# Pieces of four in place of two in the halved feed-forward blocks of a two-layer diffusion trunk

## The chip, the core and the metric

The program runs on one core of a Trainium2 chip. Its time is device microseconds (us) from start to end of one execution. The engines are TensorE (PE, with its weight loads as PEld), VectorE (DVE), ScalarE (ACT), GpSimd (POOL) and SyncE (SP); DVE, ACT, POOL and SP each take their instructions in a fixed order.

## The reference, cut to what matters

The reference is a trunk of two layers over 512 latent and 256 context tokens, 1024 wide, in float32. Each layer is a half feed-forward step, a mixer and a second half feed-forward step. Only the feed-forward step matters here:

```
def _swiglu(h, w1, w3, w2):                     # h: tokens x 1024, D_FF = 2816
    return (jax.nn.silu(h @ w1) * (h @ w3)) @ w2

x = x + 0.5 * gate * _swiglu(modulate(rmsnorm(x)), w1, w3, w2)      # the same for the context y
```

The modulation vectors (shift, scale, gate, nine per layer) are products of `silu(c)` with the columns of `w_mod`, 1024 x 9216 per layer, and need that matrix once.

## The kernel before, in words

Everything is kept transposed: features on the 128 partitions, tokens along the row. The hidden width 2816 is 22 tiles of 128, counted by `f`; the model width is 8 tiles, counted by `dt`. Each float32 product is three matmuls on high and low parts (`mm3`, lines 162 to 167): `wh` by `xh`, `wh` by `xl`, `wl` by `xh`. The parts of a weight tile come from `parts` (line 582) and `split` (line 157): a load from DRAM into a `raw` buffer (SP, line 579), a cast to `wh` on ACT, a subtraction to `wl` on DVE. There are five `raw` buffers and four pairs of `wh` and `wl`, and the weights are prepared in one fixed order, up to four tiles ahead.

Two of the four feed-forward blocks, the second of layer 0 and the first of layer 1, are "halved" (`HALVED`, line 40; `ffn_halved`, line 808). They follow each other in time. In them a hidden tile from `f` = 4 on is made by `up_halved` (line 752): seven products of 12 matmuls each, 384 columns wide, in place of eight of that size, by a scheme with sums and differences of weights (lines 611 to 618, on DVE) and of tokens (the 24 tiles `T`, slots of 512 columns that live through the whole block). ACT copies partial results out of PSUM (`half`, line 774), DVE adds them (lines 788, 795), and the two factors are multiplied and split into `g` (lines 796 to 805). Between a copy and the next product into the same PSUM tile stands one other product; the copies stand in ACT's order behind the activation of line 789, which needs DVE's line 788.

A block runs in pieces. A piece makes `n` hidden tiles (the up stage) and then multiplies them by its part of `w2` into all 8 `dt` of both token groups (the down stage). The downs of a piece stop at PSUM: ACT scales each result into a slot `xpart` (line 229) and POOL adds it in DRAM to the parked stream (`xkept`, line 231), 16 adds a piece. Only the last piece adds in SBUF. Before the change the pieces are 2 and 2 (tiles 0 to 3, not halved), seven of 2 (tiles 4 to 17), and one of 4 (tiles 18 to 21). In a down stage two `dt` of both groups, four PSUM tiles, go together: first the products with the piece's first hidden tile for all four, then with its second one, then the four evictions. The PSUM has 8 such tiles, and all activations share 45 slots (line 86).

Beside this the modulation vectors of the next use are made on DVE by `mod_chunks` (line 364), on a clock of its own that counts matmul time: one chunk of `w_mod`, 512 KB, is loaded by SP into one of two `wm` buffers (line 371) and used by four DVE instructions (`macc`, lines 319 and 321); after every four chunks DVE folds the sums (lines 329, 330). Where a chunk's instructions fall among the others on DVE is settled when the program is built, as is the order on each engine. A `raw` or `wm` load waits on SP until its buffer is free, and those behind it wait too.

Of the kernel before, what the change touches and what calls it, by code (L numbers as in the profile page):

```python
# [22 lines left out]
NF = DFF // P  # L23
PIECES = (4, 4, 4, 4, 2, 4)
# [16 lines left out]
HK, HN, SUB, WHOLE = KD // 2, NT // 2, 2, 4  # L41
# [3 lines left out]
def per_block(n):  # L45

    return 2 if n * P * 2 <= 1024 else 1
# [34 lines left out]
class Kernel:  # L82
# [443 lines left out]
    def weight_order(self):  # L526

        ins = self.ins

        def halved(l, s):  # L530
            f0 = 0
            for npc in PIECES:
                w2 = ins["w2"][l, s, :, f0 * D : (f0 + npc) * D].rearrange("p (d f n) -> p d f n", d=KD, f=npc)
                sub = npc if f0 + npc == NF else SUB
                for a in range(0, npc, sub):
                    for f in range(f0 + a, f0 + a + sub):
                        both = [ins["w13"][l, s, f, :, m * 1024 : (m + 1) * 1024] for m in range(2)]
                        if f < WHOLE:
                            yield from both
                        else:  # L540
                            yield both
                    per = 8 // sub
                    for d in range(0, KD, per):
                        yield w2[:, d : d + per, a : a + sub]
                f0 += npc

        def ffn(l, s):
            f0 = 0
            for npc in PIECES:
                for f in range(f0, f0 + npc):  # L550
                    for m in range(2):
                        yield ins["w13"][l, s, f, :, m * 1024 : (m + 1) * 1024]
                n = npc * P * per_block(npc)
                for c in range(f0 * D, (f0 + npc) * D, n):
                    yield ins["w2"][l, s, :, c : c + n]
                f0 += npc

        for l in range(DEPTH):
            yield from (halved if (l, 0) in HALVED else ffn)(l, 0)
            for i in range(4, 8) if l < DEPTH - 1 else range(4):  # L560
                yield ins["w_feat"][l, i]
            for i in range(4) if l < DEPTH - 1 else range(4, 8):
                yield ins["w_feat"][l, i]
            for i in range(4):
                yield ins["w_tok"][l, i]
            for i in (10, 11, 12, 13, 8, 9, 14, 15, 16, 17):
                yield ins["w_feat"][l, i]
            for i in range(2):
                for dt2 in range(KD // 2):
                    yield ins["w_out"][l, i, dt2]  # L570
            yield from (halved if (l, 1) in HALVED else ffn)(l, 1)
# [236 lines left out]
    def ffn_halved(self, l, s, h, starts, grps, ends, done):  # L808
        nc = self.nc
        idx = 2 * s  # L810
        accs = {}
        T = {i: [[None] * HK for _ in range(2)] for i in (2, 3, 4)}
        f0 = 0
        while f0 < NF:
            g = self.empty()
            n = SUB if f0 < NF - PIECES[-1] else PIECES[-1]
            last = f0 + n == NF
            per = 8 // n

            def load():  # L820
                for st in (CTX, LAT):
                    self.load_x(st, self.kept[st])

            if f0 < WHOLE:
                if f0 == 0:
                    ws = {f: self.w13() for f in range(n)}
                    for grp in starts[:-1]:
                        self.up(ws, range(n), h, g, grp)
                    self.need(starts[-1])
                    task = self.spawn(self.differences(h, T), 1.0)  # L830
                for f in range(n):
                    if f0:
                        ws = {f: self.w13()}
                    for grp in grps if f0 else starts[-1:]:
                        self.up(ws, [f], h, g, grp)
                if f0 + n == WHOLE:
                    self.drain(task)
                    self.first_difference(h)
            else:
                for f in range(n):  # L840
                    self.up_halved(f, h, T, g, load if last and f == n - 1 else None)
            w2 = []

            def down(dt, grp, ps, fs):
                self.products([(ps, w2[dt // per], dt % per * n * P + fs[0] * P)], g, grp, fs, fs[0] == 0, fs[-1] == n - 1)

            if last:
                w2 = [self.weights() for _ in range(KD // per)]
                for grp in ends:
                    for dt in range(KD):  # L850
                        ps = self.psum("down")[:, : grp[2]]
                        down(dt, grp, ps, range(n))
                        xd = self.xs(dt, grp)
                        nc.vector.scalar_tensor_tensor(xd, ps, self.gate(l, idx, grp[0], dt), xd, op0=ALU.mult, op1=ALU.add)
                        self.square(dt, grp, accs)
                    done(grp, accs)
            else:
                for d in range(0, KD, 2):
                    if d % per == 0:
                        w2.append(self.weights())  # L860
                    these = [(dt, grp, self.psum("down")[:, : grp[2]]) for grp in grps for dt in (d, d + 1)]
                    for fs in ((0,), (1,)):
                        for dt, grp, ps in these:
                            down(dt, grp, ps, fs)
                    for dt, grp, ps in these:
                        self.add_kept(dt, grp, ps, self.gate(l, idx, grp[0], dt))
            f0 += n
# [675 lines left out]
```

## Time and profile before

| | |
|---|---|
| time, median of 3 runs | 2588.97 us (2588.43 to 2592.09) |
| time of the profiled execution | 2592.09 us |
| its span | 2590.3 us |
| PE busy | 2529.6 us, 98% |
| DVE, ACT, POOL busy | 70%, 39%, 11% |
| second feed-forward block of layer 0, halved | 905 to 1433 us |
| first feed-forward block of layer 1, halved | 1433 to 1985 us |

PE is busy nearly all the time. A stage of the halved blocks is best read as a stretch of its own: two stretches with the same number of matmuls, one longer than the other, show what the longer one lost.

### The profile page before, as it was taken

The page shows a single profiled execution, that of the slowest core. Times are in us where ns is not written, and L with a number is a line of the kernel's source. Part 1 is how long each engine was busy: PE and PEld are TensorE (multiplying, and loading weights), DVE is VectorE, ACT ScalarE, POOL GpSimd, SP SyncE. Part 2 cuts the span into 40 slices and gives each one's busy share as a digit, 9 for nine tenths or more (in the row PEclk, how much of TensorE's full clock was granted, in tenths as well). Part 3 has the DMA queues.
Part 4 walks back from the last instruction along what each step waited for, and adds up shares of the span by engine and source line. Part 5 has one row for each costly group of instructions (what it writes and reads, how often), then busy time and mean ns, then how long its engine had stood idle before and what let it go on. Part 6 is the DMA issues. An engine that isn't in the chain of part 4 may idle for free. (4 is left out here: it accounts for less than half of the span.)

```text
span 2590.3 us, 36708 instructions
## 1 busy us (share of the span) xinstructions
PE 2529.6 (98%) x14002; PEld 2246.6 (87%) x14002; DVE 1811.2 (70%) x3390; ACT 1015.7 (39%) x1780; POOL 276.6 (11%) x316
## 2 busy tenths in 40 slices
PE   8999999999999999999999999999999999999998
PEld 4888888888888888999899889989998888888887
DVE  6957767747977677788788858758777786633345
ACT  3211211223335444555454445545544263422223
POOL 0000000000000122422320132322310001000000
PEclk9999999999999999999999999999999999999999
DMA  7533433422222745787775457776663334232231
GB/s 273 161 108 122 139 122 114 130 74 100 85 79 60 198 106 130 180 204 180 168 196 187 110 111 195 162 179 179 145 159 122 114 97 119 91 98 98 94 102 41
DMA packets 149265, 345.37 MB, mean 133 GB/s; under 512 B 15712, under 2 KB 54112, under 8 KB 149088
## 3 DMA queue, kind: packets, MB, share of 16 engines
q1 hardware_dynamic: 101088, 276.94, 32.5%
q0 software_dynamic: 44928, 61.89, 15.0%
q10 hardware_dynamic: 3072, 4.20, 0.6%
q8 instruction: 109, 1.79, 0.3%
q14 instruction: 68, 0.56, 0.1%
HBM read 263.27 MB, written 75.50 MB: 131 GB/s over the span
## 5 line engine op out<-in xcount | busy, mean ns | idle before, releaser
L159 ACT CAST wh<-raw 128x1024 fp32r<-128x1024 f32 (+1 forms) x400 | 400.7, 1004 | 863.6 <-PE up L165 329.8
L160 DVE TENSOR_TENSOR wl<-raw,wh 128x1024 fp32r<-128x1024 f32 (+1 forms) x400 | 464.3, 1164 | 338.2 <-ACT wh L159 325.3
L164 PE MATMUL up<-h,wh 128*128 128x512 f32 (+2 forms) x1920 | 663.0, 347 | 21.9 <-ACT half L774 15.7
L165 PE MATMUL up<-h,wh 128*128 128x512 f32 (+2 forms) x1920 | 662.3, 345 | 0.2
L166 PE MATMUL up<-h,wl 128*128 128x512 f32 (+2 forms) x1920 | 661.0, 345 | 0.0
L231 POOL DMA_DIRECT2D xkept<-xpart x312 | 276.4, 1550 | 1904.2 <-ACT xpart L229 1595.0
L164 PE MATMUL down<-g,wh 128*128 128x256 f32 (+1 forms) x1264 | 425.7, 345 | 8.3 <-ACT xpart L229 4.3
L165 PE MATMUL down<-g,wh 128*128 128x256 f32 (+1 forms) x1264 | 431.2, 343 | 0.0
L166 PE MATMUL down<-g,wl 128*128 128x256 f32 (+1 forms) x1264 | 428.2, 341 | 0.4 <-DVE wl L160 0.4
L164 PEld LDWEIGHTS up<-h,wh 128*128 128x128 f32 x1920 | 365.7, 191 | 59.3 <-ACT half L774 17.9
L165 PEld LDWEIGHTS up<-h,wh 128*128 128x128 f32 x1920 | 366.6, 191 | 33.1 <-DVE h L515 0.7
L166 PEld LDWEIGHTS up<-h,wl 128*128 128x128 f32 x1920 | 366.2, 191 | 31.3
L321 DVE SCALAR_TENSOR_TENSOR macc<-wm,sc,macc 128x512 f32<-128x512 f32 x462 | 320.2, 746 | 56.5 <-DMA wm<-in_w_mod_dram 56.3
L164 PEld LDWEIGHTS down<-g,wh 128*128 128x128 f32 x1264 | 236.8, 190 | 41.0 <-ACT g L159 8.3
L165 PEld LDWEIGHTS down<-g,wh 128*128 128x128 f32 x1264 | 240.5, 190 | 28.1 <-DVE g L160 1.7
L166 PEld LDWEIGHTS down<-g,wl 128*128 128x128 f32 x1264 | 239.6, 190 | 28.3 <-DVE wl L160 0.6
L229 ACT ACTIVATE xpart<-down,gate 128x256 f32<-128x256 f32 (+1 forms) x288 | 152.5, 585 | 72.1 <-PE down L166 69.9
L663 DVE TENSOR_TENSOR silu<-silu,up 128x256 f32<-128x256 f32 (+1 forms) x84 | 48.5, 579 | 159.0 <-PE up L166 159.0
L164 PE MATMUL up<-t,wh 128*128 128x384 f32 x432 | 145.2, 336 | 0.3 <-ACT half L774 0.2
L166 PE MATMUL up<-t,wl 128*128 128x384 f32 x432 | 144.4, 334 | 0.0
L165 PE MATMUL up<-t,wh 128*128 128x384 f32 x432 | 144.4, 334 | 0.0
L700 DVE SCALAR_TENSOR_TENSOR x<-down,gate,x 128x512 f32<-128x512 f32 (+1 forms) x152 | 95.0, 634 | 65.9 <-PE down L166 65.2
(210 smaller groups left out, 3298.3 us busy)
## 6 DMA issues: line engine op xcount, KB each, us to landing
raw<-in_w_dram SPq DMA_DIRECT2D x260, 512.0 KB, 3.8
wm<-in_w_mod_dram SPq DMA_DIRECT2D x128, 512.0 KB, 4.3
xkept<-xpart POOLq DMA_DIRECT2D x160, 256.0 KB, 9.3
xkept<-xpart POOLq DMA_DIRECT2D x152, 128.0 KB, 8.6
raw<-in_w_feat_dram SPq DMA_DIRECT2D x36, 512.0 KB, 3.6
xkept<-x SPq DMA_DIRECT2D x44, 256.0 KB, 3.2
x<-xkept SPq DMA_DIRECT2D x44, 256.0 KB, 6.3
wm<-in_w_mod_dram SPq DMA_DIRECT2D x32, 256.0 KB, 5.5
```

What stands on the lines that cost most here:

```text
L159: self.nc.scalar.copy(hi, src)
L160: self.nc.vector.tensor_sub(lo, src, hi.bitcast(F32))
L164: nc.tensor.matmul(out, wh, xh, start=start, stop=False, skip_group_check=shared)
L165: nc.tensor.matmul(out, wh, xl, start=False, stop=False, skip_group_check=shared)
L166: nc.tensor.matmul(out, wl, xh, start=False, stop=stop, skip_group_check=shared)
L229: self.nc.scalar.activation(part, ps, AF.Copy, scale=gate)
L231: self.nc.gpsimd.dma_start(self.kept[st][:, c0 : c0 + n], part, accum_op=ALU.add)
L321: self.nc.vector.scalar_tensor_tensor(acc[v], raw, s, acc[v], op0=ALU.mult, op1=ALU.add)
L663: nc.vector.tensor_mul(t, t, ps[f, 1])
L700: nc.vector.scalar_tensor_tensor(xd, ps, self.gate(l, idx, grp[0], dt), xd, op0=ALU.mult, op1=ALU.add)
```

## The change

The halved tiles are done in pieces of `PIECES[1:]`, that is 4, 4, 4, 2 and 4, behind the two pieces of 2 that are not halved. A block then has 7 pieces in place of 10, 6 of them with adds in DRAM in place of 9; over both blocks there are 96 evictions and 96 adds fewer. The matmuls are the same ones. In the down stage of a piece of four, the first group of products is that of the first three hidden tiles, the second that of the fourth. `weight_order` gives the weights in the new order, with `w2` in tiles of two `dt` by four `f`, which are contiguous in a row, in place of four `dt` by two `f`.

```
--- before.py
+++ after.py
@@ -531,7 +531,7 @@
             f0 = 0
             for npc in PIECES:
                 w2 = ins["w2"][l, s, :, f0 * D : (f0 + npc) * D].rearrange("p (d f n) -> p d f n", d=KD, f=npc)
-                sub = npc if f0 + npc == NF else SUB
+                sub = SUB if f0 < WHOLE else npc
                 for a in range(0, npc, sub):
                     for f in range(f0 + a, f0 + a + sub):
                         both = [ins["w13"][l, s, f, :, m * 1024 : (m + 1) * 1024] for m in range(2)]
@@ -811,9 +811,8 @@
         accs = {}
         T = {i: [[None] * HK for _ in range(2)] for i in (2, 3, 4)}
         f0 = 0
-        while f0 < NF:
+        for n in (SUB,) * (WHOLE // SUB) + PIECES[1:]:
             g = self.empty()
-            n = SUB if f0 < NF - PIECES[-1] else PIECES[-1]
             last = f0 + n == NF
             per = 8 // n
 
@@ -859,7 +858,7 @@
                     if d % per == 0:
                         w2.append(self.weights())
                     these = [(dt, grp, self.psum("down")[:, : grp[2]]) for grp in grps for dt in (d, d + 1)]
-                    for fs in ((0,), (1,)):
+                    for fs in (range(n - 1), range(n - 1, n)):
                         for dt, grp, ps in these:
                             down(dt, grp, ps, fs)
                     for dt, grp, ps in these:
```

The order of the instructions is the same as before up to the first halved tile of layer 0, and again behind the second halved block; between these it differs as follows. (From line 815 on, the changed kernel's lines are lower by one.)

On PE, in the first down stage behind halved tiles, the products with the last hidden tile begin as follows before (`g_1489` and `g_1508` hold that tile; 24 matmuls of the stage stand ahead of the first one with it):

```order
L164 MATMUL down_9672<-g_1485_9435,wh_9537 128x512
L165 MATMUL down_9672<-g_1486_9436,wh_9537 128x512
L166 MATMUL down_9672<-g_1485_9435,wl_9538 128x512
L164 MATMUL down_9629<-g_1489_9460,wh_9537 128x256
L164 MATMUL down_9630<-g_1489_9460,wh_9537 128x256
L164 MATMUL down_9631<-g_1508_9577,wh_9537 128x512
L164 MATMUL down_9632<-g_1508_9577,wh_9537 128x512
L165 MATMUL down_9629<-g_1490_9461,wh_9537 128x256
```

and with the change (`g_1538` and `g_1557` hold the fourth tile; 36 matmuls of the stage stand ahead):

```order
L164 MATMUL down_9919<-g_1534_9733,wh_9841 128x512
L165 MATMUL down_9919<-g_1535_9734,wh_9841 128x512
L166 MATMUL down_9919<-g_1534_9733,wl_9842 128x512
L164 MATMUL down_9916<-g_1538_9758,wh_9841 128x256
L165 MATMUL down_9916<-g_1539_9759,wh_9841 128x256
L166 MATMUL down_9916<-g_1538_9758,wl_9842 128x256
L164 MATMUL down_9917<-g_1538_9758,wh_9841 128x256
```

The last hidden tile is needed 36 matmuls into the stage in place of 24.

On DVE, at the start of the up stage of tile 14 in layer 0 (1239 us in the trace), before: `wl_11768` is the last weight tile of tile 14, `wm_` are chunks of `w_mod`, line 788 is the first addition for tile 14:

```order
L160 TENSOR_TENSOR wl_11768<-raw_11517,wh_11767 128x512
L319 TENSOR_SCALAR macc_11730<-wm_11476,sc 128x512
L319 TENSOR_SCALAR macc_11731<-wm_11476,sc 128x512
L321 SCALAR_TENSOR_TENSOR macc_11730<-wm_11476,sc,macc_11730 128x512
L321 SCALAR_TENSOR_TENSOR macc_11731<-wm_11476,sc,macc_11731 128x512
L321 SCALAR_TENSOR_TENSOR macc_11730<-wm_11732,sc,macc_11730 128x512
L321 SCALAR_TENSOR_TENSOR macc_11731<-wm_11732,sc,macc_11731 128x512
L321 SCALAR_TENSOR_TENSOR macc_11730<-wm_11732,sc,macc_11730 128x512
L321 SCALAR_TENSOR_TENSOR macc_11731<-wm_11732,sc,macc_11731 128x512
L160 TENSOR_TENSOR wl_11841<-raw_11565,wh_11840 128x1024
L321 SCALAR_TENSOR_TENSOR macc_11730<-wm_11803,sc,macc_11730 128x512
L788 TENSOR_TENSOR half_11785<-up_11821,half_11785 128x384
```

The same engine with the change, at the start of the up stage of tile 16 in layer 0 (of two tiles, `wl_12064` and line 788 as above):

```order
L611 TENSOR_TENSOR raw_12132<-raw_11819,raw_11821 128x512
L321 SCALAR_TENSOR_TENSOR macc_11920<-wm_12046,sc,macc_11920 128x512
L614 TENSOR_TENSOR raw_12132<-raw_11821,raw_12132 128x512
L321 SCALAR_TENSOR_TENSOR macc_11921<-wm_12046,sc,macc_11921 128x512
L321 SCALAR_TENSOR_TENSOR macc_11920<-wm_12046,sc,macc_11920 128x512
L321 SCALAR_TENSOR_TENSOR macc_11921<-wm_12046,sc,macc_11921 128x512
L160 TENSOR_TENSOR wl_12064<-raw_11742,wh_12063 128x512
L160 TENSOR_TENSOR wl_12137<-raw_11819,wh_12136 128x1024
L788 TENSOR_TENSOR half_12081<-up_12111,half_12081 128x384
```

No chunk stands between the weight tile and line 788 here; before there were two whole ones and a part of a third.

On DVE in layer 1, at the start of the up stage of tile 16 (1832 us in the trace), before:

```order
L160 TENSOR_TENSOR wl_17676<-raw_17435,wh_17675 128x512
L319 TENSOR_SCALAR macc_17599<-wm_17356,sc 128x512
L321 SCALAR_TENSOR_TENSOR macc_17598<-wm_17356,sc,macc_17598 128x512
L321 SCALAR_TENSOR_TENSOR macc_17599<-wm_17356,sc,macc_17599 128x512
L321 SCALAR_TENSOR_TENSOR macc_17598<-wm_17600,sc,macc_17598 128x512
L321 SCALAR_TENSOR_TENSOR macc_17599<-wm_17600,sc,macc_17599 128x512
L321 SCALAR_TENSOR_TENSOR macc_17598<-wm_17600,sc,macc_17598 128x512
L321 SCALAR_TENSOR_TENSOR macc_17599<-wm_17600,sc,macc_17599 128x512
L321 SCALAR_TENSOR_TENSOR macc_17598<-wm_17697,sc,macc_17598 128x512
L160 TENSOR_TENSOR wl_17749<-raw_17473,wh_17748 128x1024
L788 TENSOR_TENSOR half_17699<-up_17729,half_17699 128x384
```

and with the change at the start of the up stage of tile 12, behind `wl_16392`, its last weight tile:

```order
L319 TENSOR_SCALAR macc_16337<-wm_16114,sc 128x512
L321 SCALAR_TENSOR_TENSOR macc_16336<-wm_16114,sc,macc_16336 128x512
L321 SCALAR_TENSOR_TENSOR macc_16337<-wm_16114,sc,macc_16337 128x512
L611 TENSOR_TENSOR raw_16460<-raw_16153,raw_16155 128x512
L321 SCALAR_TENSOR_TENSOR macc_16336<-wm_16338,sc,macc_16336 128x512
L614 TENSOR_TENSOR raw_16460<-raw_16155,raw_16460 128x512
L321 SCALAR_TENSOR_TENSOR macc_16337<-wm_16338,sc,macc_16337 128x512
L321 SCALAR_TENSOR_TENSOR macc_16336<-wm_16338,sc,macc_16336 128x512
L321 SCALAR_TENSOR_TENSOR macc_16337<-wm_16338,sc,macc_16337 128x512
L321 SCALAR_TENSOR_TENSOR macc_16336<-wm_16413,sc,macc_16336 128x512
L160 TENSOR_TENSOR wl_16467<-raw_16153,wh_16466 128x1024
L788 TENSOR_TENSOR half_16415<-up_16445,half_16415 128x384
```

These two are alike: three instructions of one chunk, four of a second, one of a third, and then line 788.

## Rows read from the trace of the kernel before

**Rows 1.** The page, its first part: engine, busy us, share, instructions.

```profile
PE 2529.6 (98%) x14002; PEld 2246.6 (87%) x14002; DVE 1811.2 (70%) x3390; ACT 1015.7 (39%) x1780; POOL 276.6 (11%) x316
```

**Rows 2.** Stretches: from:to us, busy us (instructions) by engine, granted clock, DMA share, GB/s.

```profile
1032.00:1051.00 19.00, 17.05 (x97) 14.67 (x97) 16.94 (x28) 10.83 (x21) 9.76 (x12) 1.00 0.63 124
1097.50:1127.00 29.50, 29.50 (x170) 29.07 (x168) 26.25 (x42) 14.42 (x25) 4.34 (x5) 1.00 0.87 226
1127.00:1143.90 16.90, 16.90 (x98) 14.83 (x98) 15.41 (x24) 10.96 (x21) 10.58 (x12) 1.00 0.76 146
1219.80:1239.00 19.20, 17.25 (x100) 14.83 (x99) 10.75 (x26) 10.85 (x21) 9.34 (x12) 1.00 0.56 90
1239.00:1274.10 35.10, 30.94 (x169) 30.62 (x168) 26.17 (x40) 14.61 (x25) 4.89 (x6) 0.95 0.75 191
1337.60:1394.40 56.80, 56.80 (x325) 55.97 (x324) 51.02 (x80) 27.04 (x48) 4.23 (x5) 1.00 0.69 190
1589.20:1620.40 31.20, 29.77 (x170) 29.11 (x169) 21.76 (x33) 14.52 (x26) 3.08 (x4) 1.00 0.76 206
1637.50:1666.60 29.10, 29.10 (x169) 29.10 (x168) 25.53 (x39) 14.19 (x24) 4.62 (x5) 1.00 0.87 225
1683.70:1717.70 34.00, 31.06 (x170) 30.71 (x169) 22.16 (x35) 14.15 (x25) 3.16 (x4) 0.95 0.71 187
1734.80:1768.90 34.10, 31.02 (x170) 30.69 (x169) 26.34 (x40) 14.69 (x25) 3.34 (x4) 0.95 0.71 191
1832.10:1865.30 33.20, 30.91 (x169) 30.55 (x169) 25.58 (x39) 14.71 (x25) 2.89 (x4) 0.95 0.70 191
1882.30:1942.60 60.30, 58.36 (x328) 58.01 (x327) 42.81 (x78) 27.11 (x48) 3.92 (x5) 0.97 0.56 152
```

**Rows 3.** Waits of 1543 to 1985 us: who waited for whom, us, times, longest.

```profile
DVE macc L321 <- DMA wm<-in_w_mod_dram: 31.2, 8, 6.3
...
PE up L164 <- ACT half L774: 11.6, 5, 3.1
```

**Rows 4.** DVE in order of time from 1735.6 us: start, us, instruction, [idle before, releaser].

```profile
1735.61 0.69 DVE L160 TENSOR_TENSOR wl<-raw,wh 128x512 fp32r<-128x512 f32 x1 [4.66 <-ACT wh L159]
...
1737.12 4.05 DVE L321 SCALAR_TENSOR_TENSOR macc<-wm,sc,macc 128x512 f32<-128x512 f32 x6
1742.19 1.23 DVE L160 TENSOR_TENSOR wl<-raw,wh 128x1024 fp32r<-128x1024 f32 x1 [1.02 <-ACT wh L159]
1748.24 0.75 DVE L321 SCALAR_TENSOR_TENSOR macc<-wm,sc,macc 128x512 f32<-128x512 f32 x1 [4.83 <-DMA wm<-in_w_mod_dram]
```

**Rows 5.** PE in order of time, the stop in the same stage.

```profile
1750.56 0.44 PE L164 MATMUL up<-h,wh 128*128 128x384 f32 x1 [3.08 <-ACT half L774]
```

**Rows 6.** SP in order of time, its loads ahead of that stop.

```profile
1723.72 12.98 SPq L579 DMA_DIRECT2D raw<-in_w_dram  x2
1738.55 2.99 SPq L371 DMA_DIRECT2D wm<-in_w_mod_dram  x2
```

**Rows 7.** DVE in order of time at 1036 us.

```profile
1036.12 1.24 DVE L330 TENSOR_REDUCE mrow<-mturn 128x16 f32<-128x512 f32 x2
1037.28 0.55 DVE L803 TENSOR_TENSOR half<-half,half 128x384 f32<-128x384 f32 x1
```

**Rows 8.** PE in order of time at 1038 us.

```profile
1038.32 0.97 PE L164 MATMUL down<-g,wh 128*128 128x256 f32 x4 [1.95 <-ACT g L159]
```

**Rows 9.** DMA issues of 200 to 800 us: x issues, KB, median us to landing.

```profile
wm<-in_w_mod_dram SPq DMA_DIRECT2D x39, 512.0 KB, 3.5
```

**Rows 10.** DMA issues of 1543 to 1985 us.

```profile
wm<-in_w_mod_dram SPq DMA_DIRECT2D x30, 512.0 KB, 7.3
```

**Rows 11.** DMA issues of 1002.7 to 1433 us.

```profile
wm<-in_w_mod_dram SPq DMA_DIRECT2D x40, 512.0 KB, 6.6
xkept<-xpart POOLq DMA_DIRECT2D x59, 256.0 KB, 10.5
```

**Rows 12.** The page, its costliest groups: ACT's evictions of the downs.

```profile
L229 ACT ACTIVATE xpart<-down,gate 128x256 f32<-128x256 f32 (+1 forms) x288 | 152.5, 585 | 72.1 <-PE down L166 69.9
```

More of the change, by code (lines that the diff above doesn't have):

```diff
@@ L533, in halved @@
                 w2 = ins["w2"][l, s, :, f0 * D : (f0 + npc) * D].rearrange("p (d f n) -> p d f n", d=KD, f=npc)
-                sub = npc if f0 + npc == NF else SUB
+                sub = SUB if f0 < WHOLE else npc
                 for a in range(0, npc, sub):
@@ L813, in ffn_halved @@
         f0 = 0
-        while f0 < NF:
+        for n in (SUB,) * (WHOLE // SUB) + PIECES[1:]:
             g = self.empty()
-            n = SUB if f0 < NF - PIECES[-1] else PIECES[-1]
             last = f0 + n == NF
@@ L861, in ffn_halved @@
                     these = [(dt, grp, self.psum("down")[:, : grp[2]]) for grp in grps for dt in (d, d + 1)]
-                    for fs in ((0,), (1,)):
+                    for fs in (range(n - 1), range(n - 1, n)):
                         for dt, grp, ps in these:
```

## The prediction

> **What bounds the kernel now.** I read the page's engine line first, then the matmul starts of the two halved blocks stage by stage, then the waits of these blocks, and last each engine's order of time around one stop. The line says that PE is the bound: 2529.6 of 2590.3 us busy [rows 1]. DVE, at 70%, and ACT, at 39%, matter only where PE waits for them. So the change can win no more than what PE loses in the halved blocks, and the stretches show that loss. An up stage of two halved tiles is 168 matmuls. Undisturbed it takes 29.1 us (1637.5) or 29.5 us (1097.5); a down stage of 96 matmuls takes 16.9 us (1127.0) [rows 2]. Stretches with the same counts that are longer:
>
> - layer 0, downs: 19.0 - 16.9 = 2.1 us and 19.2 - 16.9 = 2.3 us; one up stage: 35.1 - 29.5 = 5.6 us;
> - layer 1, ups: 31.2 - 29.1 = 2.1; 34.0 - 29.1 = 4.9; 34.1 - 29.1 = 5.0; 33.2 - 29.1 = 4.1; and the run of four tiles at the block's end, 60.3 us against 56.8 us for the same run in layer 0: 3.5 us [rows 2].
>
> Together 29.6 us: 10.0 in layer 0, 19.6 in layer 1. There are two causes.
>
> The six long up stages each stop once, in the first tile behind a down stage, shortly before its last product. At 1750.56 PE has stood for 3.08 us for ACT's copy of line 774 [rows 5]. That copy stands on ACT behind line 789, which needs line 788 of DVE, and DVE stood 4.83 us for a chunk `wm` of the modulation weights until 1748.24 [rows 4]. In layer 1 DVE waits eight times for such chunks, 31.2 us in all, and PE five times for ACT's copy, 11.6 us [rows 3]. Of the 4.9 us lost in such a stage some 3.1 is the stop; the remaining 1.8 comes with a granted clock of 0.95 over the stage, that is with a stretch at 1.2 in place of 2.4 GHz right behind the stop [rows 2, 5]. The chunk is late because SP issued it at 1738.55, behind a pair of `raw` loads that held its queue from 1723.72 on [rows 6], and because a chunk takes 7.3 us to land here [rows 10], against 3.5 us where no adds run [rows 9]. DVE itself had been held to 1735.61 by the last weight tile, whose buffer PE frees only at the end of the down stage [rows 4], and then had two chunks in a row to do. So a down stage that ends gathers chunks, and the next up stage pays.
>
> The two long down stages wait for the second hidden tile: 1.95 us at 1038.32 [rows 8]. It was late because DVE did the folds of the modulation sums, to 1037.28, ahead of line 803, which makes it [rows 7].
>
> **The change, part by part.** *Evictions and adds.* 96 of 288 evictions go, 0.585 us each on ACT [rows 12]: 56 us of an engine that is idle 61% of the time, and 96 adds on POOL. None of it ends a wait of PE by itself, so it counts 0. The evictions run beside PE's downs; without that cover they would lengthen the down stages, and the one at 1127.0 takes its 16.9 us with 16 of them beside it [rows 2].
>
> *Fewer ends of down stages.* Behind halved tiles a block has 7 turns from down to up now (into tiles 6, 8, 10, 12, 14, 16, 18) and 4 then (8, 12, 16, 18). Which of them has chunks in DVE's order between the last weight tile and line 788 can be read from the order shown with the change. In layer 0 the turn into tile 14, with two chunks and a part of a third, cost 5.6 us. With the change no turn of layer 0 looks like it: the turn into 16 has none there, those into 8 and 18 none or a part, the one into 12 one and a half, as the turn into 12 had before without a long stage. So layer 0's 5.6 us go. In layer 1 the turns into 8 and 16 get two chunks that come behind a fold or behind weight tiles; the like before (into 14) cost nothing. The turn into 12 is the exact like of the old turn into 16, which cost 4.1 us. The turn into 18 keeps one chunk behind the last weight tile, as before, at 3.5 us, and stands behind a piece of two in both kernels.
>
> *A longer cover for the last tile.* 36 matmuls in place of 24 run before it is needed: 36 x 16.9/96 = 6.3 us in place of 4.2. The late tile at 1038.32 came 6.3 us into the stage that began at 1032.0 [rows 2, 8], so the same lateness would just be covered: 2.1 + 2.3 = 4.4 us go. If folds made it later still, each us would cost one.
>
> *Up runs of four tiles.* DVE and ACT work hardest in the up stages, and these become 58 us long. The trace holds that case: 1337.6 to 1394.4 is a run of four with chunks and folds in it, DVE busy 51.0 of 56.8 us, PE without a stop [rows 2]. Cost 0; if DVE fell behind, each run could cost what a stop costs, up to 5.0 us.
>
> *What stays.* The turn into 12 in layer 1: between 0 and 4.1 us. I take 2.0, half, because its chunk waits behind the adds of a down stage that issues them half as densely (16 in 33.8 us in place of 16 in 16.9). The turn into 18: between 0 and 3.5; I take 3.5, since the piece ahead of it is unchanged. Sum: 29.6 - 5.5 = 24.1 us less. On the profiled execution, 2592.1 us, that is 2568.0; this execution was 3.1 us above the median of the runs, so on the median 2588.97 - 24.1 = 2564.9 us.
>
> On the adds and the chunks there is a rule besides the rows. The rows say that a 512 KB chunk lands in 3.5 us without adds and in 6.6 and 7.3 us in the blocks with them [rows 9 to 11]. The Trainium skill's page "DMA: Bandwidth & Descriptors", section "Issuing engines are not separate DMA queues", says that transfers from different engines share the same 16 DMA engines and interleave; by it, adds at half density would bring the chunk at the turn into 12 about in time, and the sum would be 29.6 - 3.5 = 26.1 us. The rows bear out that chunks are slower beside adds, but they show no half density.
>
> **Rivals.** *All of it goes.* The chunks land in time at every turn, since the adds are thinner and the order has shifted: 2588.97 - 29.6 = 2559.4 us. For it: the spread from 3.5 to 7.3 us [rows 9, 10]. Against it: SP's queue still holds chunks behind `raw` loads, and that is no matter of the adds [rows 6].
>
> *The stops are only put together.* A down stage of 33.8 us gathers twice the chunks, and each turn behind a piece of four pays twice: in both layers three turns of some 4.9 us, 29.4 in all, and the time stays at about 2589. For it: DVE's order is fixed, and it is held in a down stage by weight tiles that wait for PE [rows 4]. Against it: a buffer of weights comes free every 8.4 us also within the long down stage, so DVE gets on, and the order shows no turn with more than two and a half chunks.
>
> *Too few slots; slower.* Of 45 slots `T` holds 24 and the tiles `g` of a piece of four 12, where a piece of two held 6. Nine are left for `xpart`, chunk sums and copies. A group of four evictions comes every 48 matmuls, 8.4 us, and its last one then needs a slot of the group before, some 10 us after that was issued. An add of 256 KB lands in 10.5 us [rows 11], so ACT would wait now and then, and PE from the point where an add needs more than about 18.5 us, since a PSUM tile has a further group of 8.4 us in hand. At an assumed 21 us, 2.5 us in two groups of each of six pieces, 30 us, would make it 2565 + 30 = 2595 us. Against it: half the adds per time. The Trainium skill, "Perfetto Trace Analysis", section "Optimization Strategy", says that the same gap repeating on the busy engine can mean too little memory for the next tile; it would show as a gap in each group of a long down stage. No row here shows such a gap.
>
> **How the numbers follow.** Forecast, 2 to 10 us of stops stay: 0.52. All goes, under 2 us stays: 0.25. More than 10 us stays, but still faster: 0.13. Put together, no change: 0.06. Slots, slower: 0.04. A change within 0.2%, 5 us, can't be told from none here. Faster by more than that: 0.52 + 0.25 + 0.13 = 0.90; within: 0.06; slower: 0.04. The predicted time is 2565. The range reaches down to all gone, 2559, and 3 us below for an execution without the small stops; up it takes 22 us left of 29.6, that is 2581: from 2556 to 2581.
>
> **What would show it.** Right: 192 evictions; up runs of four of 56.8 to 59 us with a clock of 1.00; down stages of four of 33.8 us, without a wait for `g`; in layer 0 no stop at a turn; in layer 1 at most two, into tiles 12 and 18, each behind a wait of DVE for `wm`; chunks landing in less than 7 us. Wrong: stops at turns that the order shows free of chunks; a wait of ACT's evictions for adds; PE waiting inside an up run of four; a wait for the fourth hidden tile; or losses outside the two blocks, where the order is unchanged.

## The result, and the profile after

The change brings 2558.13 us (median of 4 runs, 2556.99 to 2558.49) against 2588.7 us for the kernel before (4 runs beside it, 2587.02 to 2592.09): 30.6 us less, ratio 0.988 with a 95% interval of 0.9862 to 0.9897. The two profiled executions took 2592.09 and 2558.49 us, 33.6 us apart. The forecast of 2565 us was on the right side and its range holds the time, but by its size the result lies at the rival in which all of the loss goes (2559.4 us).

The engine line of the page after, which answers to [rows 1], and the evictions, which answer to [rows 12]:

```profile
PE 2513.8 (98%) x14002; PEld 2237.4 (88%) x14002; DVE 1808.8 (71%) x3390; ACT 964.0 (38%) x1684; POOL 191.1 (7%) x220
...
L229 ACT ACTIVATE xpart<-down,gate 128x256 f32<-128x256 f32 x192 | 102.5, 584 | 133.5 <-PE down L166 94.9
```

PE issues the same 14002 matmuls. 96 evictions and 96 adds are gone, as counted; the span is 33.8 us shorter, and PE's busy time, with the same matmuls, 15.8 us: so part of the gain is PE standing still less, and part is matmuls that took less time. Of these 15.8 us, 10.6 lie in the stages that ran in part at the lower clock before: the four ups at 0.95 and the run of four at 0.97 of [rows 2], and one unhalved up shown further down.

The stages of the halved blocks after, in the columns of [rows 2]. The first and third up of four of layer 0, each with its down, the last four tiles of layer 0, the three ups of four of layer 1 and its last four tiles (left out: the second up and down of layer 0, 58.5 and 33.7 us, the downs of four of layer 1, 33.7 us each, and the ups of two, 29.2 and 29.1 us):

```profile
1002.80:1061.20 58.40, 58.40 (x337) 58.23 (x336) 56.02 (x90) 28.41 (x51) 4.51 (x6) 1.00 0.63 169
1061.20:1094.90 33.70, 33.70 (x196) 29.78 (x196) 23.21 (x41) 12.87 (x23) 10.67 (x13) 1.00 0.82 170
...
1187.10:1246.00 58.90, 58.90 (x340) 58.44 (x339) 52.09 (x90) 28.62 (x50) 2.76 (x4) 1.00 0.49 139
1246.00:1279.40 33.40, 33.40 (x193) 29.50 (x193) 28.48 (x44) 13.01 (x23) 11.28 (x14) 1.00 0.86 185
...
1325.80:1382.00 56.20, 56.20 (x326) 56.20 (x325) 51.94 (x82) 27.30 (x48) 4.14 (x5) 1.00 0.70 188
1528.70:1587.00 58.30, 58.30 (x338) 58.26 (x336) 54.71 (x88) 29.00 (x50) 4.66 (x6) 1.00 0.63 167
1620.70:1679.10 58.40, 58.40 (x337) 58.21 (x336) 55.36 (x87) 29.35 (x50) 2.76 (x4) 1.00 0.56 150
1712.80:1773.10 60.30, 58.78 (x337) 58.14 (x336) 55.50 (x89) 28.47 (x51) 2.82 (x4) 1.00 0.54 145
...
1852.90:1909.30 56.40, 56.40 (x328) 56.40 (x327) 42.14 (x77) 27.25 (x48) 4.87 (x6) 1.00 0.60 161
```

In all but one of these rows PE's busy time equals the stretch, and the granted clock is 1.00. One stage stops, the up at 1712.8, the turn into tile 12 of layer 1, by 60.3 - 58.4 = 1.9 us. Its two stops, of PE in order of time:

```profile
1726.28 0.45 PE L164 MATMUL up<-h,wh 128*128 128x384 f32 x1 [0.83 <-ACT half L774]
...
1733.50 0.44 PE L164 MATMUL up<-t,wh 128*128 128x384 f32 x1 [0.69 <-ACT half L774]
```

VectorE's waits for chunks in layer 1, 1543 to 1960 us, against [rows 3], and the landings there and in layer 0 (1002.7 to 1423 us), against [rows 10, 11]:

```profile
DVE macc L321 <- DMA wm<-in_w_mod_dram: 7.3, 4, 3.0
```

```profile
wm<-in_w_mod_dram SPq DMA_DIRECT2D x29, 512.0 KB, 4.3
xkept<-xpart POOLq DMA_DIRECT2D x32, 256.0 KB, 7.2
...
wm<-in_w_mod_dram SPq DMA_DIRECT2D x40, 512.0 KB, 4.3
xkept<-xpart POOLq DMA_DIRECT2D x36, 256.0 KB, 7.9
```

31.2 us of waiting became 7.3, the longest wait 3.0 in place of 6.3 us, and a chunk lands in 4.3 us in place of 7.3 and 6.6.

### The profile page after: what moved, and what is told of

Read it like the earlier page. It is cut to its first block, busy times and chain, and to the rows that moved or that the text cites. A ratio compares the mean times of both kernels' runs of the same rounds, so it can differ in the third digit from the quotient of the medians.

```text
span 2556.5 us, 36298 instructions
## 1 busy us (share of the span) xinstructions
PE 2513.8 (98%) x14002; PEld 2237.4 (88%) x14002; DVE 1808.8 (71%) x3390; ACT 964.0 (38%) x1684; POOL 191.1 (7%) x220
## 3 DMA queue, kind: packets, MB, share of 16 engines
q1 hardware_dynamic: 91872, 276.94, 33.8%
## 5 line engine op out<-in xcount | busy, mean ns | idle before, releaser
L166 PEld LDWEIGHTS up<-h,wl 128*128 128x128 f32 x1920 | 363.0, 189 | 31.2
L321 DVE SCALAR_TENSOR_TENSOR macc<-wm,sc,macc 128x512 f32<-128x512 f32 x462 | 322.0, 746 | 24.3 <-DMA wm<-in_w_mod_dram 24.1
L231 POOL DMA_DIRECT2D xkept<-xpart x216 | 190.9, 1355 | 1956.7 <-ACT xpart L229 1941.7
L229 ACT ACTIVATE xpart<-down,gate 128x256 f32<-128x256 f32 x192 | 102.5, 584 | 133.5 <-PE down L166 94.9
```

Of the source, the lines that this page charges most:

```text
L166: nc.tensor.matmul(out, wl, xh, start=False, stop=stop, skip_group_check=shared)
L229: self.nc.scalar.activation(part, ps, AF.Copy, scale=gate)
L231: self.nc.gpsimd.dma_start(self.kept[st][:, c0 : c0 + n], part, accum_op=ALU.add)
L321: self.nc.vector.scalar_tensor_tensor(acc[v], raw, s, acc[v], op0=ALU.mult, op1=ALU.add)
```

## The experiments

My theory was that late chunks of `w_mod` hold VectorE, and through it ACT's copy and PE's up. What the change does about them was open between two causes. **T1**: it is the load of the adds that makes the chunks late. **T2**: it is how often a down stage turns into an up stage, and where chunks stand in the queues there. A third thing changed unasked: the rows of the `w2` loads are 4 KB in place of 1 KB. All ratios below are to the kernel before, run on the same chip.

**1. No chunk loads (kernel before).** In `mod_chunks`, for the two slower paces that the halved blocks use:

```
...
+            if pace > 7.0 and len(kept) == 2:
+                steps.pop(0)
+                kept.append(kept.pop(0))
+                return kept[1]
             raw = self.wide("wm").rearrange("p (k n) -> p k n", k=2)
...
+            kept.append(raw)
```

> The kernel before, in which the modulation sums of the two halved blocks load only their first two chunks of `w_mod` and then read these two again and again (the modulation is computed from the wrong rows; every VectorE add, fold and turn stays). It takes away only the loads that VectorE waits for. My theory, that late `wm` chunks hold VectorE and through it the halved up: the six long up stages fall to about 29.3 us each, 25 us less, and the two long downs of layer 0 (folds ahead of L803) keep their 4.4 us: about 2564 us. Rival A, the slots or the order on VectorE itself hold the up and a late chunk only coincides: within 5 us of the kernel before, 2584 to 2589 us.

Measured: 2565.82 us, before 2590.56, ratio 0.9908 (0.9892 to 0.9925): 24.7 us less. The stretches of that run, in the columns of [rows 2]: the two downs of layer 0 that were long, then the up of layer 0 that was and two of the five of layer 1 (the others take 29.1 us):

```profile
1031.90:1050.90 19.00, 17.04 (x98) 14.68 (x97) 17.58 (x30) 10.81 (x21) 10.65 (x12) 1.00 0.64 103
1219.50:1238.70 19.20, 17.25 (x100) 14.87 (x99) 10.80 (x26) 10.79 (x21) 9.28 (x12) 1.00 0.57 88
1238.70:1267.90 29.20, 29.20 (x170) 29.16 (x170) 26.13 (x40) 14.58 (x25) 4.99 (x6) 1.00 0.71 159
...
1720.40:1749.50 29.10, 29.10 (x169) 29.10 (x168) 26.11 (x40) 14.56 (x25) 3.34 (x4) 1.00 0.64 152
1858.80:1915.20 56.40, 56.40 (x328) 56.40 (x327) 41.23 (x76) 27.18 (x48) 3.52 (x5) 1.00 0.56 146
```

The ups are whole, with VectorE just as busy as before (its order differs in 53 of 3390 places); the downs are still 19.0 and 19.2 us. So the chunks' part of the loss, 25.2 us, is shown, the 4.4 us of the downs are apart from it, and rival A falls. That folds make these 4.4 us rests on [rows 7, 8]: no run took the folds away.

**2. Half the adds (kernel before).** In `add_kept` and `ffn_halved`:

```
...
+        if add:
+            self.nc.gpsimd.dma_start(self.kept[st][:, c0 : c0 + n], part, accum_op=ALU.add)
...
-                        self.add_kept(dt, grp, ps, self.gate(l, idx, grp[0], dt))
+                        self.add_kept(dt, grp, ps, self.gate(l, idx, grp[0], dt), f0 < WHOLE or f0 // 2 % 2 == 0)
```

> The kernel before, in which every second halved piece of two tiles evicts its products but doesn't add them into the kept x by DMA (the output lacks these products). ScalarE's evictions, the downs, the pieces and the w2 loads stay; the adds of the halved pieces are half as many, as in the change. Theory T1, the DMA load of the adds makes the chunks land late: landings of `wm` fall from 7 us to about 4.5 us and at least 15 of the 25 us go: 2564 to 2574 us. Theory T2, what counts is how often a down stage turns into an up stage and where the chunks stand in SP's and VectorE's order there: the landings move by under 1 us and at most 8 us go: 2580 to 2589 us.

Measured: 2578.14 us, ratio 0.9957 (0.9941 to 0.9973): 12.4 us less, between both expectations. The stages say why. The pieces without adds are those of tiles 6, 10 and 14, so the ups of tiles 8, 12 and 16 follow a down stage without adds. The ups of that run that were long before, into tile 14 of layer 0 and into 6, 10, 12, 16 and 18 of layer 1:

```profile
1239.30:1274.50 35.20, 31.02 (x170) 30.69 (x169) 26.22 (x40) 14.62 (x25) 3.30 (x4) 0.95 0.69 184
1589.50:1620.60 31.10, 29.66 (x169) 29.02 (x168) 21.72 (x33) 14.48 (x25) 3.03 (x4) 1.00 0.77 207
1684.00:1717.20 33.20, 31.01 (x170) 30.68 (x169) 22.11 (x35) 14.11 (x25) 3.13 (x4) 0.95 0.72 192
1734.30:1763.40 29.10, 29.10 (x169) 29.10 (x168) 26.08 (x40) 14.77 (x25) 0.00 (x0) 1.00 0.51 163
1826.60:1856.10 29.50, 29.37 (x169) 29.05 (x168) 25.61 (x39) 14.60 (x25) 0.00 (x0) 1.00 0.50 161
1873.10:1931.90 58.80, 56.95 (x327) 56.31 (x326) 42.81 (x78) 27.04 (x48) 3.67 (x5) 1.00 0.57 155
```

Only the two that follow a down stage without adds are whole, to 0.4 us (POOL issues no add in them); the stages of 14, 6 and 10 are within 0.8 us of what they were, and that of 18 is 1.5 us shorter. A stop is made by the adds of the down stage just ahead of it. It is no matter of a block's average: in layer 0 the median landing fell to 4.3 us, and the 6 us lost behind a down with adds stayed.

**3. No adds (kernel before).** The same edit with `f0 < WHOLE` alone.

> The kernel before, in which no halved piece of two adds its products into the kept x (the output lacks all of them); evictions, downs, turns and loads stay. With every second piece's adds left out, the stops went behind just the down stages that had none and stayed behind the others. If the adds of the down stage ahead are the whole cause: the stops at the up stages of before (25 us) all go, and 2560 to 2567 us is left. If the number of turns has a cost of its own, as the run in two passes suggests (half the turns at the same adds gave most of the gain): some stops stay, 2568 to 2576 us.

Measured: 2564.98 us, before 2589.93, ratio 0.9895 (0.9879 to 0.9912): 25.0 us less, the same as without chunk loads. VectorE's waits for chunks from 1000 to 1985 us, in the kernel before 51.6 us in 16 times, and the landings (1002.7 to 1433, then 1543 to 1985 us):

```profile
DVE macc L322 <- DMA wm<-in_w_mod_dram: 6.6, 6, 2.4
```

```profile
wm<-in_w_mod_dram SPq DMA_DIRECT2D x40, 512.0 KB, 3.5
...
wm<-in_w_mod_dram SPq DMA_DIRECT2D x29, 512.0 KB, 4.3
```

No halved up stage stops, with all fourteen turns from down to up in place; in this run and in run 2 the 3390 instructions of VectorE stand in the very order of before. The two long downs still wait, 1.95 and 2.23 us. A turn has no price of its own; it is where the adds and the chunks collide, and taking away either side gives the same 25 us.

**4. Few turns, all adds.** The change with the downs of a four in two passes of two tiles:

```
...
-                for d in range(0, KD, 2):
...
+                for c in range(0, n, 2):
+                    w2.clear()
+                    for d in range(0, KD, 2):
...
+                            self.add_kept(dt, grp, ps, self.gate(l, idx, grp[0], dt))
```

> The change, with the downs of each halved piece of four tiles done in two passes of two tiles, each pass with its own evictions and adds: as many evictions, adds and w2 loads of the same shape as the kernel before, but the up and down stages alternate as seldom as in the change. T1 (the load of the adds makes the chunks late): the landings of `wm` are again about 7 us and 10 to 25 us come back: 2570 to 2585 us. T2 (the number of turns and what stands in SP's queue at them): within 6 us of the change, 2556 to 2564 us.

Measured: 2568.25 us, ratio 0.9918 (0.9903 to 0.9933): 10 us above the change, 22 below the kernel before. With adds as dense as before, but half the turns behind them, about a third of the gain is lost. Three of its turns stop, into tile 12 in both layers and into 16 in layer 1. The up into tile 12 of layer 1:

```profile
1719.50:1781.30 61.80, 58.83 (x337) 58.16 (x336) 55.52 (x89) 28.55 (x51) 4.67 (x6) 1.00 0.63 168
```

It loses 61.8 - 58.4 = 3.4 us, where the change loses 1.9, and VectorE waits 4.44 us for a chunk in it, where the change waits 3.00. In layer 0 it is something else. ScalarE of that run in order of time, and PE behind it:

```profile
1186.32 0.69 ACT L229 ACTIVATE xpart<-down,gate 128x512 f32<-128x512 f32 x1 [1.29 <-DMA xkept<-xpart]
1190.38 0.47 ACT L229 ACTIVATE xpart<-down,gate 128x256 f32<-128x256 f32 x1 [3.36 <-DMA xkept<-xpart]
...
1194.63 0.48 ACT L776 COPY half<-up 128x384 f32<-128x384 f32 x1
```

```profile
1195.16 0.69 PE L164 MATMUL up<-t,wh 128*128 128x384 f32 x1 [3.19 <-ACT half L776]
```

ScalarE's evictions wait, one after the other, for a slot that an earlier `xpart` holds until its add has landed; the last of them are still there 6 us into the up stage, and the copy that PE wants stands behind them. This is the rival of too few slots, which I had as a mechanism of the change: 32 adds in one long down stage bring it about, the change's 16 don't. The rule of the Trainium skill that I set beside that rival ("Perfetto Trace Analysis", section "Optimization Strategy") says that the same gap, repeating on the engine that should be saturated, can mean too little memory for the next tile. Here five evictions in a row wait, but on ScalarE; PE, the saturated engine, shows one stop of 3.19 us.

**5. Longer rows of `w2` (kernel before),** laid out so that a load of a piece of two is contiguous:

```
...
-                    for d in range(0, KD, per):
-                        yield w2[:, d : d + per, a : a + sub]
+                    n = 8 * P
+                    for c in range((f0 + a) * D, (f0 + a + sub) * D, n):
+                        yield ins["w2"][l, s, :, c : c + n]
...
+    for l, s in HALVED:
+        w2[l, s] = np.concatenate(pieces, 3)[l, s]
```

> The kernel before, with the down weights of the halved tiles laid out in memory so that each load of a piece of two takes rows of 4 KB in place of 1 KB; nothing else moves. In the change these rows became 4 KB too, without anything in the prediction that counts on it. If the short rows load the DMA engines so that chunks land late, landings of `wm` fall towards 4.3 us and 10 us or more go: under 2579 us. If they don't matter, as my prediction has it: 2586 to 2592 us.

Measured: 2582.82 us (9 runs, 2577.52 to 2585.35), ratio 0.9967 (0.9956 to 0.9978): 7.7 us less, between both. What the turn into tile 14 of layer 0 loses went from 6.0 to 1.9 us, into tile 10 of layer 1 from 4.9 to 2.7 us; the turn into 12 moved by 1.2 us, that into 16 by nothing (33.4 us):

```profile
1240.50:1271.50 31.00, 29.72 (x169) 29.04 (x168) 25.98 (x40) 14.56 (x25) 4.91 (x6) 1.00 0.83 216
1678.50:1710.30 31.80, 29.66 (x169) 29.02 (x168) 22.05 (x35) 14.02 (x25) 3.08 (x4) 1.00 0.75 201
1727.40:1760.30 32.90, 31.02 (x169) 30.66 (x169) 26.20 (x40) 14.73 (x25) 3.29 (x4) 0.95 0.73 196
```

The median landings stayed at 6.5 and 7.3 us, so how shorter rows lengthen just these stops stays open.

**6. Few turns, all adds, longer rows.** Runs 4 and 5 together.

> The change with the downs of each halved four in two passes of two tiles, as the earlier run that came out at 2568 us, but with the down weights of halved tiles laid out so that the loads take rows of 4 KB as in the change. What is left against the change is then the doubled evictions and adds alone. That run lost 10 us to the change. If the short rows of the `w2` loads made it (layout alone took 8 us off the kernel before): 2557 to 2561 us. If the doubled adds made it: 2565 to 2570 us. Both in part: between.

Measured: 2567.11 us, ratio 0.9915 (0.99 to 0.993), against 0.9918 with short rows. Where the turns are few, the rows' length is worth nothing that can be told; the 9 to 10 us between this run and the change come with the doubled adds and the evictions that go with them.

**7. The change again, and without groups.** The change itself, timed a second time:

> The change itself, unaltered, timed beside the next three on one chip: 2556 to 2560 us, ratio to the kernel before 0.988.

Measured: 2558.23 us, ratio 0.9883 (0.9866 to 0.9899). Then, in its downs:

```
-                    for fs in (range(n - 1), range(n - 1, n)):
+                    for fs in (range(n),):
```

> The change, with the down products of a piece no longer grouped: each output tile is finished before the next, so the last `g` tile is wanted after 9 matmuls (three in a piece of two) in place of 36 (24). My step held that the grouping is why the first downs of a piece of four never wait: in the change the last `g` tile was written 3.4 to 5.2 us after the last up matmul, and 36 matmuls last 6.3 us. If so, each of the ten halved and unhalved pieces that are not a block's last loses 2 to 3.5 us: 2578 to 2595 us. Rival: the products of the other tiles' passes or TensorE's queue cover it anyway, 2556 to 2564 us.

Measured: 2559.03 us, ratio 0.9883 (0.9868 to 0.9898), the same as the change: my expectation was wrong by 19 us or more. The instruction order of this kernel shows why, at the first down of the unhalved pieces (the hidden tiles are `g0_1311` and `g0_1316` with their low parts `g1`):

```
L164 MATMUL down_1323_8617<-g0_1316_8605,wh_1269_8278 128x512
L164 MATMUL down_1324_8618<-g0_1311_8548,wh_1269_8278 128x512
L165 MATMUL down_1324_8618<-g1_1312_8549,wh_1269_8278 128x512
L165 MATMUL down_1323_8617<-g1_1317_8606,wh_1269_8278 128x512
```

The code asks for all products of `down_1323` ahead of those of `down_1324`. The order that is settled when the program is built has put the first products of 1324 ahead of the one that needs the late low part `g1_1317`. So this way of writing the loops is not what covers the last tile.

**8. No chunk loads in the change.** The edit of run 1 in the changed kernel.

> The change, in which the modulation sums of the halved blocks load only their first two chunks of `w_mod` and read these again and again (the modulation is computed from the wrong rows). It shows what late chunks still cost in the change. By my step, one turn (into tile 12 of layer 1): 2 us, 2556 us. If late chunks still delay other work that no matmul gap shows, or if the loads themselves slow the adds and evictions: 2548 to 2554 us. If nothing: 2558 us.

Measured: 2557.95 us, ratio 0.9869 (0.9854 to 0.9883): the stop into tile 12 is gone from the trace, and the time is the change's within what can be told. So by the trace late chunks cost the change the 1.9 us at 1712.8, and by the times nothing that shows.

**9. Chunks issued from ScalarE (kernel before).**

```
-            nc.sync.dma_start(raw, self.ins["w_mod"][steps.pop(0)])
+            (nc.scalar if pace > 7.0 else nc.sync).dma_start(raw, self.ins["w_mod"][steps.pop(0)])
```

> The kernel before, with the chunks of the two halved blocks' modulation sums issued from ScalarE in place of SP, so that no `raw` load stands ahead of them in the issuing engine's order; bytes, adds and turns stay. If the chunks are late because they are issued behind `raw` loads that wait for a buffer: 10 us or more go, under 2579 us. If they are late because the transfers themselves are slow beside the adds: within 6 us of the kernel before. Rival: ScalarE stands at the wait for the `wm` buffer ahead of its copies and evictions: slower than before, 2595 us or more.

Measured: 2595.38 us, ratio 1.0019 (1.0008 to 1.003): slower by 5 us. The landings of the two blocks, and two waits of 1000 to 1985 us:

```profile
wm<-in_w_mod_dram ACTq DMA_DIRECT2D x40, 512.0 KB, 6.6
...
wm<-in_w_mod_dram ACTq DMA_DIRECT2D x30, 512.0 KB, 7.2
```

```profile
DVE macc L321 <- DMA wm<-in_w_mod_dram: 50.0, 13, 6.7
PE up L164 <- ACT half L774: 18.2, 13, 2.3
```

The chunks take as long to land as from SP [rows 10, 11], VectorE waits for them as long (50.0 us; 51.6 in the kernel before), and PE's stops are more and shorter. The edit also moved the built order: VectorE's order differs in 240 of 3390 places, and ScalarE stands at the wait for a buffer, so the 5 us are not the issuer's price alone.

Of the two reasons that I gave for a late chunk, the slow landing beside adds is left standing. The other, that SP issues it behind `raw` loads [rows 6], was misread, and the trace of the kernel before shows how. The buffer that the late chunk takes is read last by the second of the six chunk instructions from 1737.12 [rows 4], which ends at about 1737.12 + 4.05 x 2/6 = 1738.47 us; SP issues the chunk at 1738.55. At all six long ups the issue comes within 0.1 us of that end. So the chunk starts late because there are two `wm` buffers and VectorE, held by the last weight tile, gets to the old chunk late. No run gave the chunks a third buffer.

The Trainium skill's "DMA: Bandwidth & Descriptors", section "Issuing engines are not separate DMA queues", says that transfers run on the same 16 DMA engines and interleave, whichever engine issued them. The trace agrees: 6.6 us before and 6.6 us here.

**10. The first piece as a four as well.** The change, with the four unhalved tiles, which it leaves as two pieces of two, in one piece:

```
-                sub = SUB if f0 < WHOLE else npc
+                sub = npc
...
-        for n in (SUB,) * (WHOLE // SUB) + PIECES[1:]:
+        for n in PIECES:
...
```

> The change, and beside it the first piece of the two halved blocks (four unhalved tiles, which the change leaves as two pieces of two) done as one piece of four. Two down stages and 32 evictions with their adds go. In the change these four stages (from 930, 982, 1456 and 1508 us) lose 2.2, 4.1, 2.2 and 4.1 us to late evictions and a lower clock. If the load on ScalarE by the split of the differences makes the evictions late whatever the pieces, one stop a block stays: 4.4 us gained, about 2554 us. If the stops go with the stages: 12.6 us, about 2546 us. Rival: the differences get less time beside matmuls and hold the first halved up: 2558 to 2570 us.

Measured: 2545.74 us (2544.6 to 2547.28), ratio 0.9833 (0.9818 to 0.9847): 12.5 us below the change, faster than both kernels. In the change, the unhalved up, down, up and down of layer 0:

```profile
904.50:929.60 25.10, 25.10 (x122) 21.06 (x121) 22.29 (x36) 13.15 (x21) 0.00 (x0) 1.00 0.20 64
929.60:948.60 19.00, 17.26 (x98) 14.55 (x96) 15.02 (x26) 10.79 (x20) 7.10 (x8) 1.00 0.58 102
948.60:982.00 33.40, 33.40 (x192) 29.62 (x193) 15.55 (x26) 11.09 (x20) 7.10 (x8) 1.00 0.48 101
982.00:1002.80 20.80, 18.64 (x97) 15.88 (x96) 11.27 (x20) 11.72 (x22) 9.77 (x11) 0.92 0.55 106
```

The same work in this run, in layer 0 (layer 1 takes the same 58.4 and 33.4 us):

```profile
905.60:964.00 58.40, 58.40 (x315) 50.57 (x314) 47.57 (x81) 25.48 (x43) 0.00 (x0) 1.00 0.20 64
964.00:997.40 33.40, 33.40 (x193) 29.51 (x192) 16.01 (x26) 13.76 (x24) 11.25 (x14) 1.00 0.66 102
```

25.1 + 19.0 + 33.4 + 20.8 = 98.3 us became 58.4 + 33.4 = 91.8 us, 6.5 us a block, with the clock at 1.00 throughout. In the change PE stops twice in these stages of each block, 1.74 and 2.16 us, for evictions by ScalarE; in this run it does not.

## Why the prediction was right, and where it was not

**What bounds the kernel** was right: the gain is stops of PE in the two blocks. Of the 29.6 us read from the stages, 27.7 are gone (1.9 are left, at 1712.8). The split into chunks (25.2) and folds (4.4) was measured on one side: the chunks' part is 24.7 to 25.0 us in runs 1 and 3, with the two long downs left as they were.

**Fewer ends of down stages** was right in its count of what goes, with the wrong weight on its reasons. I read stops off the place of chunks in VectorE's order and SP's queue. Runs 2 and 3 show that the place is only the occasion: with the same order and no adds ahead, the same turns don't stop. And the place in SP's queue was misread: the late chunk waits for its buffer, not behind `raw` loads (run 9).

**The turn into 12 of layer 1** was forecast to keep 2.0 us, for the thinner adds, and keeps 1.9. The reason is borne out by run 4, where the same turn with adds as dense as before loses 3.4 us. That it would be just half was a guess, and that it came so near is luck.

**The turn into 18 of layer 1** is the term that was mis-sized: 3.5 us forecast, nothing measured (56.4 us against 56.8 in [rows 2] for an undisturbed run). I took "one chunk behind the last weight tile, as before, behind the same piece of two" for the same case. VectorE at that turn, before and then after:

```profile
1886.95 2.08 DVE L321 SCALAR_TENSOR_TENSOR macc<-wm,sc,macc 128x512 f32<-128x512 f32 x3 [6.26 <-DMA wm<-in_w_mod_dram]
...
1895.41 0.55 DVE L788 TENSOR_TENSOR half<-up,half 128x384 f32<-128x384 f32 x1
```

```profile
1857.52 0.75 DVE L321 SCALAR_TENSOR_TENSOR macc<-wm,sc,macc 128x512 f32<-128x512 f32 x1 [1.49 <-DMA wm<-in_w_mod_dram]
...
1862.12 0.55 DVE L788 TENSOR_TENSOR half<-up,half 128x384 f32<-128x384 f32 x1
```

The late chunk is there 4.6 us after the up began in both (1882.3 and 1852.9). But before, eight chunk instructions stand between that landing and line 788, and after, four: line 788 starts 13.1 us into the stage before, and 9.2 us after. At the turn into 12 it starts 11.9 us in, and PE waits 0.83 us. The six long ups of the kernel before obey the same sum: line 788 starts 15.3, 12.5, 14.1, 14.2, 13.5 and 13.1 us in, and PE's stop is 4.16, 1.32, 2.94, 3.08, 2.29 and 1.94 us, each time what is above 11.1 to 11.2 us. What had to be counted was the work between the chunk that lands late and line 788, not the chunks behind the last weight tile.

**A longer cover** came out right in the time, by luck: the two waits for a hidden tile are gone, but not by the cover. In the two long downs line 803 started 5.3 us into the stage, behind the folds [rows 7]. In the change the built order puts folds ahead of line 803 at one of the eight downs with adds behind halved tiles, that of the piece of two at 1835.9:

```profile
1837.96 1.24 DVE L330 TENSOR_REDUCE mrow<-mturn 128x16 f32<-128x512 f32 x2
1839.11 0.55 DVE L803 TENSOR_TENSOR half<-half,half 128x384 f32<-128x384 f32 x1
```

There line 803 starts 3.2 us in, and PE does not wait, with 24 matmuls for cover. In the downs of four it starts 1.4 to 3.0 us in, and in [rows 7, 8] PE has the tile 1.0 us behind that start; so the 4.2 us of 24 matmuls would have done there, by estimate, as well. Whether 36 matmuls would have covered a tile as late as that of [rows 7] was not tried, and run 7 shows that the grouping makes no cover that the built order would not make.

**Evictions, adds and up runs at 0**: for the evictions and the up runs right, since run 3 keeps every eviction and wins the 25 us, and no run of four lost anything by itself (56 of 58.4 us of VectorE in the busiest). For the adds too little: as work of POOL they count nothing, but as load beside the chunks they were one side of the cause, and I gave that weight only at the turn into 12. Their halving per us of a down stage, with that of the evictions, is worth 9 to 10 us beside the fewer turns (runs 4 and 6), by chunks and by slots.

**The size.** On the medians 30.6 us went where 24.1 were forecast, 6.5 more; on the profiled executions 33.6, 9.5 more, since the one before was 3.1 us above its median. Of the 9.5, 3.5 are the turn into 18. 1.5 are an unhalved up of layer 1 that ran at a lower clock for a part before and not after, before and then after:

```profile
1487.30:1522.20 34.90, 34.90 (x192) 31.11 (x193) 15.63 (x26) 11.11 (x20) 7.07 (x8) 0.95 0.46 98
```

```profile
1474.50:1507.90 33.40, 33.40 (x192) 29.62 (x193) 15.54 (x26) 11.08 (x20) 7.10 (x8) 1.00 0.53 106
```

These 1.5 us are not put down to the change: PE's stop ahead of this stage is 1.74 us in both, and among runs of the kernel before the same stage is at 1.00 in the traces of runs 3 and 5 and at 0.95 in that of run 2. Some 3.9 are tenths spread over the stages. The halved tiles of layer 0 took 391.7 us before (1002.7 to 1394.4) and 379.2 after, 12.5 less where 10.0 were forecast; those of layer 1 took 399.6 (1543.0 to 1942.6) and 380.6, 19.0 less where 14.1 were, the 3.5 of the turn into 18 among them. I had taken the shortest stages as the norm, and most undisturbed ones were a little above it. Some 0.6 I don't assign.

**The rivals.** All goes: nearly, for both of its reasons, the thinner adds and, at the turn into 18, the shifted order; what I held against it, chunks behind `raw` loads, was the misreading. Only put together: fell, the turns behind long downs cost 1.9 us in all. Too few slots: not in the change, but run 4 shows it, on ScalarE as described, where the adds are twice as many.

## What to carry to other kernels

When an engine waits for a load, look for what shares the DMA engines in the stretch just ahead, not at the load's median: leave that traffic out in every second stage, and see which stops go. Hold the load's issue against the moment its buffer came free before blaming the queue. Two edits that each remove the same whole loss (no chunks, no adds) have found one collision, not two costs. Larger pieces pay where the loss is at a piece's end, whatever makes it; then look at every piece, also those that the change leaves out: the four unhalved tiles, where evictions came late, gave another 12.5 us.

## What the runs showed of the hardware

A 512 KB load lands, at the median, in 3.5 and 4.3 us (layers 0 and 1) with no accumulating adds behind the halved tiles (run 3), in 4.3 us with 16 adds in a down stage of 33.7 us (the change), and in 6.6 and 7.3 us with 16 in one of 16.9 us [rows 10, 11]. Issued from ScalarE it took 6.6 and 7.2 us (run 9). So the median of layer 1 is the same with thin adds as with none.

Behind some stops of PE the granted clock was at the lower of its two levels, 1.2 GHz, for a stretch (0.95 over the stage at 1734.8, behind 3.08 us [rows 2, 5]), which made some 5 us of a 3 us stop. The length of the stop alone does not tell when: the clock fell behind stops of 2.29 us (the up at 1832.1, 0.95 [rows 2]) and of 1.74 us (the unhalved up at 1487.3), and stayed up behind one of 2.28 us (run 4, the up at 1719.5, 1.00) and the one of 1.95 us of [rows 8] (the down at 1032.0, 1.00).

The length of the rows of a load, 1 KB or 4 KB, was worth 7.7 us in one order of the same work and nothing that can be told in another.
